# Layer 0's gate and up projections by seven block products instead of eight, and the down projection in groups of three tiles

## The chip, the cores and the metric

The kernel runs on one core of one Trainium2 chip. The metric is the device time of one execution in microseconds, the median of three runs. The engines are TensorE (PE, the matmuls), VectorE (DVE), ScalarE (ACT), GpSimd (POOL) and SyncE (SP), whose queue starts the DMA transfers.

## What is computed

Two layers of a diffusion backbone on 512 latent tokens (x) and 256 context tokens (ctx), 1024 features, all in fp32. Layer 0 is an RG-LRU and short-convolution mixer and a ConvFFN, on both streams; layer 1 is a neighbourhood attention and a ConvFFN, on x. The part that is changed is layer 0's ConvFFN; its input is a modulated copy of each stream, and its result is gated by a modulation vector:

```python
m_x = [t[:, None, :] for t in jnp.split(sc_c @ mod_w[i] + mod_b[i], 6, axis=-1)]
...
def conv_ffn(h, w_gate, w_up, conv_w, conv_b, w_down):
    g = dwconv(h @ w_gate, conv_w, conv_b, FFN_CONV // 2, FFN_CONV // 2)
    return (jax.nn.silu(g) * (h @ w_up)) @ w_down
```

`w_gate` and `w_up` are 1024 x 2816, `w_down` is 2816 x 1024, the convolution is over three neighbouring tokens and per feature. `mod_w` is 1024 x 6144 per layer: 24 chunks of 256 columns, times a vector for x and one for ctx.

## The kernel before, in words

**Products.** Activations lie with features on partitions and tokens on the free axis: 768 columns, x (XS, 512) before ctx (CS, 256). Every product in fp32 is three matmuls of rounded parts (`mm3`, lines 300 to 303): high weights by high activations, high by low, low by high. Of activations `hh` and `hl` are the high and the low part, of an FFN tile's result the two halves of `a`.

**Weights.** All weights are a list of units in the order of use (`unit`, `dma_to`, `split_w`, `split_to`, `use`, lines 109 to 167). A unit is loaded by SP into one of three raw buffers (`raw`, 128x1024), cast to its high part `wh` by ACT (L129), and the low part `wl` is the difference, taken by DVE (L130). There are four pairs of `wh` and `wl`. A load is issued as soon as the unit three before it has been split. Only SP's order is that of the code; the other engines' orders are set by a scheduler when the program is built.

**Layer 0's FFN.** The 2816 inner features are 22 tiles of 128 (f0 to f21). `ffn0_tile` (from line 848) does one: the gate's product (8 blocks of 128 rows x 3 matmuls, of 512 and of 256 columns), the convolution (ACT L838, DVE L839 and L840 from PSUM), silu (L841), the up product and the multiplication with it (L860), and the split of the result into `a` (ACT L845, DVE L846). Tiles 0 and 1 run apart, under the layer norm that precedes. The tiles are grouped, `FG0 = [7, 5, 3, 7]`: when a group and one more tile are done, the group's rows of `w_down` are multiplied for all eight panels of 128 output features, and `resid` (L731) adds each into the residual. The last group goes by column segments through `passes`, so that the next layer norm can start.

**Modulation.** The chunks are computed beside other work. `mod_step` (from line 200) does single steps: DVE multiplies 128x256 weights by a vector and adds (L220, L222); for ctx, where it is needed (all of layer 0, chunks 0 to 7 of layer 1), ACT multiplies (L224) and POOL adds (L226). PE then transposes the sums (L197), DVE reduces (L189). `mod_pe` (from line 252) does a chunk on PE instead, with the weights as the moving side (L240) and two transposes (L262); it serves in the mixer, with buffers of its own (`a`, L277). `mod_q` is the list of chunks that are still to do. In the kernel before, layer 0's chunks 8 to 19 go through `mod_pe` in the mixer, its chunks 20 to 23 and all 24 of layer 1 through `mod_step` in the FFN.

**Mixer.** For j = 0 to 3 it takes five products in the order sg, gates, sx, gr, sb, then the output projection. `seven_tile` and its helpers exist only after the change.

## Time and profile before

| what | value |
|---|---|
| median of 3 runs | 1605.63 us (1604.83 to 1608.91) |
| the profiled execution | 1607.75 us, its span 1605.9 us |
| mean granted TensorE clock | 0.996 |
| layer 0's FFN, tile 3 to the last down group | 371 to 822 us |
| last down group, norms, first projections of layer 1 | 822 to 930 us |
| attention | 930 to 1190 us |
| layer 1's output projection, norms and FFN | 1200 to 1606 us |

The span runs from the first instruction to the last. Busy time is time in which an engine has an instruction running; the matmuls overlap in the records, so their cadence is read from their starts. Where PE is busy for a whole stretch, only less work on PE shortens it. The stretches were found by the tiles' names in the timeline.

### The profile page before, as it was taken

The numbers are of one execution on the slowest core, as the hardware profiler recorded it, in microseconds if no ns is written. First come the engines' busy times: TensorE is split into PE (matmuls) and PEld (weight loads), VectorE is DVE, ScalarE is ACT, GpSimd is POOL, SyncE is SP. The second block draws the span as 40 slices with busy tenths as digits, with TensorE's granted clock in tenths as the row PEclk, the third lists the DMA queues.
The fourth block names the chain that finished last, engine by engine and source line by source line (L and its number), as shares of the span: only waits on it lengthen the run. The fifth ranks groups of instructions, "written<-read, shape, count | busy, mean of one in ns | idle before, by whom it ended". The sixth has DMA issues, their size and how long they took to land.

```text
span 1605.9 us, 24813 instructions
## 1 busy us (share of the span) xinstructions
PE 1560.7 (97%) x9630; PEld 1383.0 (86%) x9630; DVE 1050.3 (65%) x1899; ACT 757.5 (47%) x1329; POOL 297.2 (19%) x319
## 2 busy tenths in 40 slices
...
GB/s 280 248 146 100 151 79 145 157 77 171 138 112 135 134 111 160 121 165 87 60 104 143 104 79 66 53 73 44 50 150 120 100 94 95 92 92 105 99 99 53
DMA packets 284086, 184.27 MB, mean 115 GB/s; under 512 B 6720, under 2 KB 273344, under 8 KB 283968
## 3 DMA queue, kind: packets, MB, share of 16 engines
...
HBM read 180.56 MB, written 2.10 MB: 114 GB/s over the span
## 4 chain that ended last, share of the span: by engine, by line
PE 86%; DVE 4%; POOL 3%; ACT 2%; DMA 2%; issue 2%; SPq 0%; POOLq 0%; ACTq 0%; DVEq 0%
PE ps L302 22%; PE ps L301 22%; PE ps L303 22%; PE ps L1421 2%; PE ps L1423 2%; PE ps L1422 2%; PE ps L1059 2%; POOL sq L773 2%; PE ps L959 1%; PE ps L960 1%; PE ps L958 1%; DMA xk<-in_x_dram 1%; PE ps L240 1%; PE ps L1081 1%; PE ps L1074 1%
## 5 line engine op out<-in xcount | busy, mean ns | idle before, releaser
L301 PE MATMUL ps<-hh,wh 128*128 128x256 f32 (+1 forms) x1200 | 402.7, 336 | 0.0
L302 PE MATMUL ps<-hl,wh 128*128 128x256 f32 (+1 forms) x1200 | 400.4, 334 | 0.2 <-DVE hl L795 0.2
L303 PE MATMUL ps<-hh,wl 128*128 128x256 f32 (+1 forms) x1200 | 400.1, 334 | 0.3 <-DVE wl L130 0.3
L129 ACT CAST wh<-raw 128x1024 fp32r<-128x1024 f32 (+5 forms) x214 | 209.8, 983 | 370.4 <-PE ps L302 245.8
L130 DVE TENSOR_TENSOR wl<-raw,wh 128x1024 fp32r<-128x1024 f32 (+5 forms) x214 | 257.1, 1203 | 101.3 <-ACT wh L129 100.2
L301 PEld LDWEIGHTS ps<-hh,wh 128*128 128x128 f32 x1200 | 228.3, 190 | 25.7 <-issue 2.9
L303 PEld LDWEIGHTS ps<-hh,wl 128*128 128x128 f32 x1200 | 228.4, 190 | 23.2 <-DVE wl L130 0.5
L302 PEld LDWEIGHTS ps<-hl,wh 128*128 128x128 f32 x1200 | 228.5, 190 | 22.4 <-DVE hl L795 0.6
L301 PE MATMUL ps<-a,wh 128*128 128x256 f32 (+1 forms) x632 | 196.8, 312 | 0.2 <-ACT a L660 0.2
L302 PE MATMUL ps<-a,wh 128*128 128x256 f32 (+1 forms) x632 | 194.5, 308 | 0.7 <-DVE a L662 0.7
L303 PE MATMUL ps<-a,wl 128*128 128x256 f32 (+1 forms) x632 | 194.2, 307 | 0.8 <-DVE wl L130 0.7
L301 PE MATMUL ps<-h1h,wh 128*128 128x512 f32 (+1 forms) x384 | 142.2, 373 | 2.0 <-ACT h1h L792 2.0
L302 PE MATMUL ps<-h1l,wh 128*128 128x512 f32 (+1 forms) x384 | 142.0, 372 | 0.3 <-DVE h1l L795 0.2
L303 PE MATMUL ps<-h1h,wl 128*128 128x512 f32 (+1 forms) x384 | 142.0, 371 | 0.0
L303 PEld LDWEIGHTS ps<-a,wl 128*128 128x128 f32 x632 | 121.2, 192 | 7.0 <-DVE wl L130 1.4
L301 PEld LDWEIGHTS ps<-a,wh 128*128 128x128 f32 x632 | 121.3, 192 | 6.9 <-ACT wh L129 0.8
L302 PEld LDWEIGHTS ps<-a,wh 128*128 128x128 f32 x632 | 121.3, 192 | 5.9 <-DVE a L662 0.9
L222 DVE SCALAR_TENSOR_TENSOR mr<-mw,svec,mr 128x256 f32<-128x256 f32 x196 | 110.5, 567 | 3.7
L226 POOL TENSOR_TENSOR mr<-mr,mw 128x256 f32<-128x256 f32 x84 | 72.2, 860 | 111.8 <-ACT mw L224 106.0
L1046 POOL TENSOR_SCALAR s<-s,sm 128x512 f32<-128x512 f32 x64 | 47.8, 749 | 215.8 <-DVE sm L1045 196.7
L301 PEld LDWEIGHTS ps<-h1h,wh 128*128 128x128 f32 x384 | 71.9, 188 | 14.6 <-ACT h1h L792 2.1
L302 PEld LDWEIGHTS ps<-h1l,wh 128*128 128x128 f32 x384 | 72.0, 188 | 13.3 <-DVE h1l L795 0.9
...
## 6 DMA issues: line engine op xcount, KB each, us to landing
raw<-in_w_gate_dram SPq DMA_DIRECT2D x44, 512.0 KB, 4.3
raw<-in_w_up_dram SPq DMA_DIRECT2D x44, 512.0 KB, 4.0
...
a<-in_mod_w_dram SPq DMA_DIRECT2D x24, 512.0 KB, 5.2
raw<-in_w_out_dram SPq DMA_DIRECT2D x24, 512.0 KB, 4.2
raw<-in_w_qkv_dram SPq DMA_DIRECT2D x24, 512.0 KB, 3.8
raw<-in_w_down_dram SPq DMA_DIRECT2D x22, 512.0 KB, 3.6
```

Of the source, the lines that this page charges most:

```text
L129: nc.scalar.copy(h[:, :k], raw)
L130: nc.vector.tensor_tensor(out=l[:, :k], in0=raw, in1=f(h[:, :k]), op=ALU.subtract)
L222: stt(out=a[:, 0, :], in0=w, scalar=svec[:, k, 0:1], in1=a[:, 0, :], op0=ALU.mult, op1=ALU.add)
L226: G.tensor_tensor(out=a[:, 1, :], in0=a[:, 1, :], in1=w, op=ALU.add)
L301: mm(acc, wh, rh, start=first, stop=False)
L302: mm(acc, wh, rl, start=False, stop=False)
L303: mm(acc, wl, rh, start=False, stop=last)
L773: G.tensor_tensor(out=sq[0], in0=sq[0], in1=sq.pop(m - 1), op=ALU.add)
L1046: G.tensor_scalar(out=s, in0=s, scalar1=sm[:, 2:3], scalar2=0.0, op0=ALU.mult, op1=ALU.add)
L1059: nc.tensor.transpose(p[:, 128 * j:128 * j + 128], s[:, 128 * i:128 * i + 128], ident)
L1421: mm(p, ah, u["h"][:, k % 2, :], start=k == 0, stop=False)
L1422: mm(p, ah, u["l"][:, k % 2, :], start=False, stop=False)
```

## The change

**Seven products.** From tile 3 (`SW0`) on, a tile's gate and up products are taken as one block product: two halves of the 1024 input features, two outputs (gate and up), two halves of 384 tokens (`NH`). Eight block products give that plainly; Winograd's form of Strassen's method needs seven, of sums of blocks. Each is four `mm3` with 384 columns.

- Sums of weights are made by POOL (`sums_up`, L374 to L377) in four adds of 128x512, in place in the gate's and up's raw buffers and in `z`; two more units per tile, without a load, are split from them (512 and 1024 columns). The gate's raw buffer is held (`held=3`) until the last of them is split.
- Sums of activations are made once (`seven_acts`) in tiles 0 to 2: POOL adds high and low parts, DVE takes sums and low parts, ACT casts.
- The seven products are put together by DVE (L1043, seven adds of 128x384) and one ACT copy (L1045) into `g` and `up`.
- Convolution, silu and the product with `up` (`tail0`, from L1068) come one tile later, from SBUF, the product on POOL (L1084).

**Down groups.** `FG0 = [3, 3, 3, 3, 3, 7]`; a unit of `w_down` holds three blocks of 256 columns, two panels. In the last group the first three ctx panels do all tiles but the last first (`heads`).

**Modulation.** Chunks 20 to 23 of layer 0 go to PE in the mixer's last block (j = 3), their weights through the raw buffers; chunks 16 to 23 of layer 1 go into the attention loop.

```diff
-FG0 = [7, 5, 3, 7]
+FG0 = [3, 3, 3, 3, 3, 7]
+SW0 = 3
+NH = T // 2
...
+    def mod_unit(l, i, q):
+
+        unit(mod_w[l, q * 512:(q + 1) * 512, i * 256:(i + 1) * 256].rearrange("(k p) c -> p k c", p=128), 4, 256, held=1 << 20)
+        units[-1]["plain"] = True
...
-        while state["dma"] < min(n, len(units)) and state["dma"] - 3 < state["split"]:
+        while state["dma"] < min(n, len(units)):
             u = units[state["dma"]]
-            t = rawp.tile([128, 1024], F32, tag="raw", name="raw")
-            u["raw"] = t[:, :u["a"] * u["b"]].rearrange("p (a b) -> p a b", b=u["b"])
-            nc.sync.dma_start(out=u["raw"], in_=u["src"])
+            if u["src"] is not None:
+                if len(loaded) >= 3 and loaded[-3]["rel"] >= state["split"]:
+                    break
+                t = rawp.tile([128, 1024], F32, tag="raw", name="raw")
+                u["raw"] = t[:, :u["a"] * u["b"]].rearrange("p (a b) -> p a b", b=u["b"])
+                nc.sync.dma_start(out=u["raw"], in_=u["src"])
+                loaded.append(u)
...
+            if j == 3:
+                for q in range(2):
+                    mod_unit(0, 20 + LASTMOD.index(k), q)
...
+        def sums_up(u):
+            g = units[i]
+            z = Tp.tile([128, 512], F32, tag="mr", name="z", bufs=2)
+            units[i + 2]["raw"] = z.rearrange("p (a b) -> p a b", b=128)
+            G.tensor_tensor(out=z, in0=quarter(u, 0), in1=quarter(u, 1), op=ALU.add)
+            G.tensor_tensor(out=quarter(u, 0), in0=quarter(g, 0), in1=quarter(u, 0), op=ALU.subtract)
+            G.tensor_tensor(out=quarter(g, 0), in0=z, in1=quarter(g, 0), op=ALU.subtract)
+            G.tensor_tensor(out=quarter(g, 1), in0=quarter(g, 1), in1=quarter(g, 0), op=ALU.subtract)
+            units[i + 3]["raw"] = g["raw"]
+
+        for w, held, make in ((w_gate, 3, None), (w_up, 0, sums_up)):
+            unit(w[l][:, t * 128:(t + 1) * 128].rearrange("(k p) c -> p k c", p=128), KT, 128, make=make, held=held)
+        unit(None, 4, 128)
+        unit(None, KT, 128)
...
-        for sg in SEGS if gi == len(groups0) - 1 else ((CS, XS),):
-            for m in range(8):
-                order1.append(("d", gi, m, sg))
+        if gi < len(groups0) - 1:
+            order1 += [("d", gi, m) for m in range(0, 8, 2)]
+        else:
+            order1 += [("e", gi, m) for _ in SEGS for m in range(8)]
     for o in order1:
         if o[0] == "f":
-            gu_units(0, o[1])
+            (gu_units if o[1] < SW0 else seven_units)(0, o[1])
+            continue
+        a, n = groups0[o[1]]
+        if o[0] == "d":
+            unit(w_down[0][a * 128:(a + n) * 128, o[2] * 128:(o[2] + 2) * 128].rearrange("(k p) c -> p k c", p=128), n, 256)
...
+        if j < 3:
+            mod_pe(not (k == "sb" and j > 1))
+        else:
+            mod_raw(use(2, la=1))
...
+    gate_cols(0, 5, 5)
...
+                    for q, k in enumerate(order[:-1]):
+                        mm3(p[:, 0:s[1] - s[0]], u["h"][:, k, :], u["l"][:, k, :], rh(k, *s), rl(k, *s), q == 0, False)
+                    heads[m] = u, p
+                    if m == 0:
+                        last()
...
+        for k in range(4):
+            fa, fb = Tt("fa"), Tt("fb")
+            G.tensor_tensor(out=fa, in0=f(hh[:, k, :]), in1=f(hl[:, k, :]), op=ALU.add)
+            G.tensor_tensor(out=fb, in0=f(hh[:, k + 4, :]), in1=f(hl[:, k + 4, :]), op=ALU.add)
+            tt(out=t1[:, k, :], in0=fa[:, hi], in1=fa[:, lo], op=ALU.subtract)
+            tt(out=fa[:, hi], in0=fb[:, hi], in1=fa[:, hi], op=ALU.subtract)
+            tt(out=fb[:, hi], in0=fb[:, hi], in1=t1[:, k, :], op=ALU.subtract)
+            tt(out=fb[:, lo], in0=fb[:, lo], in1=fb[:, hi], op=ALU.subtract)
+            for j, src in ((3, fa[:, hi]), (2, fb[:, hi]), (4, fb[:, lo])):
+                nc.scalar.copy(dst(j, 0, k), src)
+                tt(out=dst(j, 1, k), in0=src, in1=f(dst(j, 0, k)), op=ALU.subtract)
+            yield
...
-    mod_q.extend([(0, i, 0) for i in range(20, 24)] + [(1, i, 0) for i in range(24)])
-    ring1 = (3, lambda: Tt("mw"), 3)
+    mod_q.extend((1, i, 0) for i in range(16))
+    ring1 = (2, lambda: Tt("mw"), 3)
...
+        def product(u, q, j):
+            p = bank()[:, 0:n]
+            for k in range(4):
+                mm3(p, u["h"][:, 4 * q + k, :], u["l"][:, 4 * q + k, :], B[j](0, k), B[j](1, k), k == 0, k == 3)
+            return p
+
+        def add(o, x, y):
+            tt(out=o, in0=x, in1=y, op=ALU.add)
+
+        nc.scalar.copy(g[:, lo], product(ua, 0, "11"))
+        split_to(i0 + 4)
+        between(0)
+        p3 = product(ub, 0, 3)
+        between(1)
+        p1 = product(ud, 0, 1)
+        split_to(i0 + 5)
+        between(2)
+        add(g[:, hi], product(uc, 0, 2), g[:, lo])
+        add(up[:, lo], p3, g[:, hi])
+        add(up[:, hi], p1, up[:, lo])
+        add(g[:, hi], p1, g[:, hi])
+        between(3)
+        add(g[:, lo], product(ua, 1, "21"), g[:, lo])
+        split_to(i0 + 6)
+        between(4)
+        add(up[:, lo], product(ub, 1, 4), up[:, lo])
+        split_to(i0 + 7)
+        between(5)
+        add(g[:, hi], product(uc, 1, "22"), g[:, hi])
+        between(6)
...
+    def tail0(t, g, up, segs=(XS, CS)):
+        tap = Tt("tap")
+        if len(segs) == 2 and segs[0] == XS:
+            act(out=tap, in_=g, func=AF.Identity, scale=col("fcw0", 22 + t), bias=col("fcb0", t))
+        else:
+            for o, e in segs:
+                act(out=tap[:, o:e], in_=g[:, o:e], func=AF.Identity, scale=col("fcw0", 22 + t), bias=col("fcb0", t))
+        yield
+        for k, (do, so) in ((0, (1, 0)), (44, (0, 1))):
+            for o, e in segs:
+                stt(out=tap[:, o + do:e - so], in0=g[:, o + so:e - do], scalar=col("fcw0", k + t), in1=tap[:, o + do:e - so], op0=ALU.mult, op1=ALU.add)
...
+            act(out=tap[:, o:e], in_=tap[:, o:e], func=AF.Silu)
+        yield
+        for o, e in parts:
+            (G if segs[0] == XS else V).tensor_tensor(out=up[:, o:e], in0=tap[:, o:e], in1=up[:, o:e], op=ALU.mult)
+        yield
+        a = atile[t] = ytile()
+        for o, e in parts:
+            nc.scalar.copy(a[:, 0, o:e], up[:, o:e])
+            tt(out=a[:, 1, o:e], in0=up[:, o:e], in1=f(a[:, 0, o:e]), op=ALU.subtract)
...
+            if not (t == NF - 2 and tail_at[0] == 5):
+                tail_step(1)
+                tail_at[0] += 1
+            if i % 2 == 0 and i < 6:
+                mod_step(1, *ring1)
...
+            u = use(la=2 if it[2] == 6 else 1)
+            for j in range(2):
+                ps_ = proj({"a": n, "h": u["h"][:, :, 128 * j:128 * j + 128], "l": u["l"][:, :, 128 * j:128 * j + 128]}, (CS, XS),
+                           lambda k, o, e: atile[a0 + k][:, 0, o:e], lambda k, o, e: atile[a0 + k][:, 1, o:e])
+                tail_step(2)
+                mod_step(2, *ring1)
+                for s, p in zip((CS, XS), ps_):
+                    resid(it[2] + j, s, 5, p)
...
-    gate_cols(1, 5, 5)
-    vecs(0, 1, col("g1_1", 0, 8), col("b1_1", 0, 8), 1, 3, 1)
...
+    mod_mem[0] = lambda: mop.tile([128, 1, 256], F32, tag="ma", name="ma", bufs=1)
+    ring2 = (1, lambda: mop.tile([128, 512], F32, tag="mw", name="mw", bufs=1), 2)
+    mod_q.extend((1, i, 0) for i in range(16, 24))
...
+            mod_step(1 + (n % 4 == 0), *ring2)
...
+    mods_flush()
+    gate_cols(1, 5, 5)
+    vecs(0, 1, col("g1_1", 0, 8), col("b1_1", 0, 8), 1, 3, 1)
```

**DVE, in a tile of layer 0's FFN.** First the kernel before, one tile from the gate's convolution to the next tile's split (`wl`: low part of weights, `ps`: PSUM, `tap`: the tile's gate):

```order
L839 SCALAR_TENSOR_TENSOR tap_5386<-ps_5393,colt_72,tap_5386 128x511
L840 SCALAR_TENSOR_TENSOR tap_5386<-ps_5393,colt_72,tap_5386 128x511
L839 SCALAR_TENSOR_TENSOR tap_5386<-ps_5418,colt_72,tap_5386 128x255
L840 SCALAR_TENSOR_TENSOR tap_5386<-ps_5418,colt_72,tap_5386 128x255
L130 TENSOR_TENSOR wl_5621<-raw_5391,wh_5620 128x1024
L860 TENSOR_TENSOR tap_5386<-tap_5386,ps_5473 128x512
L860 TENSOR_TENSOR tap_5386<-tap_5386,ps_5498 128x256
L189 TENSOR_REDUCE M1_77<-ps_5523 128x4
L220 TENSOR_SCALAR mr_5604<-mw_5457,svec_75 128x256
L248 SCALAR_TENSOR_TENSOR M1_77<-M1_77,colt_72 128x4
L130 TENSOR_TENSOR wl_5695<-raw_5471,wh_5694 128x1024
L846 TENSOR_TENSOR a_5539<-tap_5386,a_5539 128x768
```

After the change, a seven-product tile that follows another (`g_5229` and `up_5230` are its outputs; `raw_5192` and `raw_5249` hold the gate and up weights of the tile after it, `a_5367` is the result of the tile before it). All subtractions of L148 belong to the next tile:

```order
L148 TENSOR_TENSOR wl_5287<-raw_5192,wh_5286 128x1024
L268 SCALAR_TENSOR_TENSOR M1_77<-M1_77,colt_72 128x4
L1043 TENSOR_TENSOR g_5229<-ps_5300,g_5229 128x384
L1089 TENSOR_TENSOR a_5367<-up_5089,a_5367 128x768
L1043 TENSOR_TENSOR up_5230<-ps_5258,g_5229 128x384
L1043 TENSOR_TENSOR up_5230<-ps_5273,up_5230 128x384
L1043 TENSOR_TENSOR g_5229<-ps_5273,g_5229 128x384
L1043 TENSOR_TENSOR g_5229<-ps_5318,g_5229 128x384
L148 TENSOR_TENSOR wl_5338<-raw_5249,wh_5337 128x1024
L1043 TENSOR_TENSOR up_5230<-ps_5349,up_5230 128x384
L148 TENSOR_TENSOR wl_5364<-z_5332,wh_5363 128x512
L1043 TENSOR_TENSOR g_5229<-ps_5370,g_5229 128x384
```

A tile now has four weight subtractions where it had two, and the next up weights' low part (`wl_5338`) stands behind five adds and the low part of `a`; the fourth subtraction follows right after these rows.

**POOL, in the same stage.** Before, only modulation adds:

```order
L226 TENSOR_TENSOR mr_5142<-mr_5142,mw_5015 128x256 x2
L226 TENSOR_TENSOR mr_5142<-mr_5142,mw_5080 128x256 x3
L226 TENSOR_TENSOR mr_5142<-mr_5142,mw_5140 128x256 x2
L226 TENSOR_TENSOR mr_5290<-mr_5290,mw_5208 128x256 x2
L226 TENSOR_TENSOR mr_5290<-mr_5290,mw_5280 128x256 x3
```

After the change, around one seven-product tile (`up_4367` is the product of a tile's tail, `z` and `raw` are sums of weights):

```order
L1084 TENSOR_TENSOR up_4367<-tap_4529,up_4367 128x768
L374 TENSOR_TENSOR z_4610<-raw_4527 128x512
L375 TENSOR_TENSOR raw_4527<-raw_4470,raw_4527 128x512
L245 TENSOR_TENSOR mr_4575<-mr_4575,mw_4534 128x256
L376 TENSOR_TENSOR raw_4470<-z_4610,raw_4470 128x512
L245 TENSOR_TENSOR mr_4575<-mr_4575,mw_4534 128x256
L377 TENSOR_TENSOR raw_4470<-raw_4470 128x512
L245 TENSOR_TENSOR mr_4575<-mr_4575,mw_4534 128x256
L1084 TENSOR_TENSOR up_4508<-tap_4686,up_4508 128x768
```

The weight sums stand between a tail's product and the next one, and modulation adds between them.

**SP, at the end of the mixer (j = 3).** Before, the chunks' weights (`a`) come between the panels of `w_in` up to chunk 19, and the queue ends with three panels:

```order
L120 DMA raw<-in_w_in_dram 128x8x128
L277 DMA a<-in_mod_w_dram 128x4x256 x2
L120 DMA raw<-in_w_in_dram 128x8x128
L120 DMA raw<-in_gates_dram 128x512
L277 DMA a<-in_mod_w_dram 128x4x256 x2
L120 DMA raw<-in_w_in_dram 128x8x128
L277 DMA a<-in_mod_w_dram 128x4x256 x2
L120 DMA raw<-in_w_in_dram 128x8x128 x2
L120 DMA raw<-in_w_out_dram 128x8x128 x24
```

After the change:

```order
L133 DMA raw<-in_mod_w_dram 128x4x256
L304 DMA a<-in_mod_w_dram 128x4x256 x2
L133 DMA raw<-in_mod_w_dram 128x4x256
L304 DMA a<-in_mod_w_dram 128x4x256 x2
L133 DMA raw<-in_gates_dram 128x512
L133 DMA raw<-in_w_in_dram 128x8x128
L133 DMA raw<-in_mod_w_dram 128x4x256 x2
L133 DMA raw<-in_w_in_dram 128x8x128
L133 DMA raw<-in_mod_w_dram 128x4x256 x2
L133 DMA raw<-in_w_in_dram 128x8x128
L133 DMA raw<-in_mod_w_dram 128x4x256 x2
L133 DMA raw<-in_w_out_dram 128x8x128 x24
```

Between the last panels of `w_in`, and ahead of `w_out`, stand eight loads of modulation weights into the same raw buffers.

## Rows read from the trace of the kernel before

**Rows 1.** The page: busy time of each engine.
```profile
PE 1560.7 (97%) x9630; PEld 1383.0 (86%) x9630; DVE 1050.3 (65%) x1899; ACT 757.5 (47%) x1329; POOL 297.2 (19%) x319
```

**Rows 2.** Windows: stretch, its length, busy us of each engine, clock, DMA share.
```profile
160.00:235.00 75.00, 74.35 (x462) 63.90 (x462) 44.53 (x69) 48.51 (x65) 12.32 (x6) 1.00 0.38 109
342.00:371.00 29.00, 29.00 (x201) 27.08 (x200) 20.77 (x30) 18.34 (x29) 7.72 (x10) 1.00 0.57 173
371.00:822.00 451.00, 451.00 (x2626) 399.43 (x2625) 296.43 (x524) 152.07 (x241) 65.33 (x77) 1.00 0.40 122
...
930.00:1190.00 260.00, 257.25 (x1784) 237.49 (x1783) 179.09 (x471) 177.45 (x422) 47.15 (x63) 1.00 0.24 70
```

**Rows 3.** PE timeline, a down panel: start, duration of one (overlapping), instruction.
```profile
500.02 0.39 PE L301 MATMUL ps<-a,wh 128*128 128x512 f32 x1
...
502.06 0.28 PE L301 MATMUL ps<-a,wh 128*128 128x256 f32 x1
...
504.58 0.40 PE L301 MATMUL ps<-a,wh 128*128 128x512 f32 x1
```

**Rows 4.** PE timeline, mixer: a modulation chunk by the row method.
```profile
172.56 0.38 PE L262 MATMUL ps<-ident,mrw 128*128 128x128 f32 x2
172.87 1.07 PE L240 MATMUL ps<-a,mvec 128*32 128x256 f32 x16
173.87 0.50 PE L301 MATMUL ps<-hh,wh 128*128 128x512 f32 x1
```

**Rows 5.** DVE timeline where POOL is idle: subtractions of 1024 and 768 columns.
```profile
662.67 1.22 DVE L130 TENSOR_TENSOR wl<-raw,wh 128x1024 fp32r<-128x1024 f32 x1
663.80 0.95 DVE L846 TENSOR_TENSOR a<-tap,a 128x768 fp32r<-128x768 f32 x1
```

**Rows 6.** POOL timeline, then DVE's over the same stretch.
```profile
367.28 10.51 POOL L226 TENSOR_TENSOR mr<-mr,mw 128x256 f32<-128x256 f32 x10 [1.36 <-ACT mw L224]
369.35 1.76 DVE L130 TENSOR_TENSOR wl<-raw,wh 128x1024 fp32r<-128x1024 f32 x1
371.04 1.84 DVE L222 SCALAR_TENSOR_TENSOR mr<-mw,svec,mr 128x256 f32<-128x256 f32 x2
...
375.38 1.81 DVE L130 TENSOR_TENSOR wl<-raw,wh 128x1024 fp32r<-128x1024 f32 x1 [1.18 <-ACT wh L129]
377.12 1.49 DVE L846 TENSOR_TENSOR a<-tap,a 128x768 fp32r<-128x768 f32 x1
```

**Rows 7.** Groups by line and shape: count, busy us, mean ns, idle before.
```profile
L222 DVE SCALAR_TENSOR_TENSOR mr<-mw,svec,mr 128x256 f32<-128x256 f32 x196 | 110.5, 567 | 3.7
...
L226 POOL TENSOR_TENSOR mr<-mr,mw 128x256 f32<-128x256 f32 x84 | 72.2, 860 | 111.8 <-ACT mw L224 106.0 <-POOL mr L226 0.4 <-DMA mw<-in_mod_w_dram 0.3
...
L129 ACT CAST wh<-raw 128x1024 fp32r<-128x1024 f32 x154 | 160.9, 1048 | 275.3 <-PE ps L302 163.4 <-PE ps L1423 77.1 <-issue 20.0
...
L840 DVE SCALAR_TENSOR_TENSOR tap<-ps,colt,tap 128x511 f32<-128x511 f32 x44 | 32.9, 748 | 1.2
...
L586 POOL TENSOR_TENSOR ri<-ri,xc 128x768 f32<-128x768 f32 x8 | 14.8, 1846 | 139.2 <-ACT ri L629 139.0
...
L860 DVE TENSOR_TENSOR tap<-tap,ps 128x512 f32<-128x512 f32 x20 | 13.7, 683 | 22.4 <-PE ps L303 22.4
...
L840 DVE SCALAR_TENSOR_TENSOR tap<-ps,colt,tap 128x255 f32<-128x255 f32 x22 | 10.5, 479 | 0.4
...
L860 DVE TENSOR_TENSOR tap<-tap,ps 128x256 f32<-128x256 f32 x20 | 8.4, 420 | 34.0 <-PE ps L303 33.5 <-ACT mw L224 0.5
...
L1375 POOL TENSOR_TENSOR R<-R,gb 128x512 f32<-128x512 f32 x3 | 3.9, 1295 | 339.7 <-ACT R L1374 339.7
```

**Rows 8.** The page: DMA issues, KB each, median us to landing.
```profile
raw<-in_w_up_dram SPq DMA_DIRECT2D x44, 512.0 KB, 4.0
```

138 lines of the change are left out of this document (114 added, 24 removed).

## The prediction

> **What bounds the kernel now.** I read the page's busy line first, then the windows by stage, then single instructions. TensorE (PE) is busy 1560.7 of 1605.9 us [rows 1], so time goes only if PE gets less work, and comes back only if PE is made to wait. The windows show where there is room for waiting [rows 2]. From 371 to 822 us, which is layer 0's FFN from tile 3 to the start of its last down group, PE is busy 451.00 of 451.00 us. VectorE (DVE) is busy 296.4 of them, ScalarE (ACT) 152.1, GpSimd (POOL) 65.3. So the stage is PE's alone, with a third of DVE spare. In the attention (930 to 1190) PE has 257.3 of 260 us and DVE 179.1. The median of the three runs is 1605.63 us; the profiled run took 1607.75 us, 2.1 more. I make the sum against the profiled run and take 2.1 off at the end. About 0.3% (4.8 us) is what a measurement here can tell from no change.
>
> **What PE saves.** The cadence of matmuls is read from their starts [rows 3]. Nine of 512 columns start from 500.02 to 502.06: 0.2267 us each. The 21 of 256 columns from 502.06 to 504.58 take 0.120 each. A tile of gate and up has 48 of each: 48 x (0.2267 + 0.120) = 16.64 us. A seven-product tile has 7 x 4 x 3 = 84 matmuls of 384 columns. No 384 is in the trace. Priced per column like a 256 it takes 0.180, like a 512 0.170, and the mean of the two rows is 0.1734; I take the mean, since the row pair is a straight line with an offset, and 384 lies halfway. A tile is then 84 x 0.1734 = 14.57 us and saves 2.07; 19 tiles (3 to 21) save 39.3 us (ends: 28.9 and 44.8). The down products keep their number: 15 tiles x 8 panels x 3 x (0.2267 + 0.120) before and after.
>
> **What else moves on PE.** Twelve modulation chunks leave this stage. The four of layer 0, chunks 20 to 23, had 16 transposes here, the eight of layer 1, chunks 16 to 23, also 16; at 0.12 us, as for a matmul of 256, that is 3.8 us less. Four chunks go into the mixer's last block by the row method, 2 transposes 0.31 us and 16 narrow matmuls 1.00 us each [rows 4]: 4 x 1.31 = 5.2 more. The other eight take their 1.9 us into the attention. Net PE gain: 39.3 + 3.8 - 5.2 - 1.9 = 36.0 us. That is the gross term; the rest is what the new work makes PE wait.
>
> **The order on DVE inside a run of seven-product tiles.** This is the term I weigh most. DVE now splits four weight tiles per tile and adds seven products. Prices: the 1024 subtraction 1.22 us and the 768 subtraction 0.95 with POOL quiet [rows 5]; in a stretch where POOL ran ten adds back to back, 1.76 to 1.81 and 1.49 [rows 6]. An add of 384 from PSUM lies between 0.42 and 0.68 (256 and 512) [rows 7]: 0.55. In the order shown above, between the low parts of the next gate weights and of the next up weights stand an add, the previous tile's low part of 768, and four adds. There are four weight buffers, and the next gate weights take the one that product 5 reads. Set the tile's start to 0: product 5 ends at 5 x 2.08 = 10.4. The ACT cast takes 1.05 [rows 7], to 11.45; the gate's low part ends at 12.7, in time for 14.57. Then 0.55 + 0.95 + 4 x 0.55 + 1.22 brings the up weights' low part to 17.6. PE wants it in the third matmul of the next tile's product 2, at 14.57 + 2.08 + 0.35 = 17.0: 0.6 us late. At the prices with POOL busy the same walk ends at 19.2, 2.2 late. What is late there is late again at the next such boundary, since the walk starts from product 5. That order stands at seven boundaries (one in each of four runs of three, three in the last run); 1.3 each is 9 us, ends 4 and 15. Six boundaries without the 768 cost 0 to 0.7 each, 1 us together. I take 10 us.
>
> **Start of tile 3.** The sums of activations are new: POOL 8 adds of 128x768, DVE 32 passes of 384, ACT 16 casts, all in tiles 0 to 2. A 768 add on POOL takes 1.85 us [rows 7], so 14.8 us; 32 x 0.53 is 17 us of DVE. In 342 to 371, DVE has 8.2 of 29.0 us idle and POOL 21.3 [rows 2]. The work is spread over about two such windows, so the last sums should end near the start of tile 3, but POOL must then still make its four weight sums (4 x 1.3 us by the 512 add in [rows 7]) before products 2 to 4 of that tile. I take 6 us of PE waiting, ends 0 and 15.
>
> **The mixer's last block.** Each chunk's two 512 KB pieces now stand on the sync queue between the input panels, in three raw buffers, and are held until their rows are computed. A load lands in about 4 us [rows 8]; a panel lasts 24 x (0.2267 + 0.120) = 8.3 us of PE. That leaves one panel's time for two pieces and the next panel: tight, not late. The window is full now (74.35 of 75.0) [rows 2], so each late piece shows. I take 1.5 us, ends 0 and 6.
>
> **Attention.** Eight chunks bring 64 steps on DVE at 0.57 [rows 7], 36 us on 179 of 260. DVE is then at 83%, in a stage in which PE waits 2.7 us now. I take 3 us, ends 0 and 10. One microsecond more stands for the modulation columns and vectors that are now finished right behind the attention. The heads of the last down group (54 matmuls of 256, 6.5 us) cover tile 21's tail; a free cover, nothing in the sum.
>
> **Sum.** -36.0 + 10 + 6 + 1.5 + 3 + 1 = -14.5 us: 1607.75 - 14.5 = 1593.2 as a profiled run, about 1591 as the median.
>
> **POOL beside DVE.** What the rows show: in 367.28 to 377.79 POOL's ten adds and DVE's subtractions both ran, POOL at 1.05 us an add, DVE at 1.76 to 1.81 instead of 1.22 [rows 5, 6]. So the two slow each other, by 40 to 50%. The Trainium skill, "SBUF — State Buffer" (section "SBUF: two separate sides"), says that a DVE operation with two SBUF inputs and a GpSimd operation that reads SBUF take one port pair as an exclusive lock, and that the loser fully blocks. The rule speaks against this change, which gives POOL four weight sums and a product per tile; the sum by it would be that of the lesser form of rival 1, the sum by the rows is the one above. The trace agrees that the two lose together: in those 10.5 us POOL did ten adds (8.6 us at their mean of 0.86) and DVE two long subtractions and two modulation passes among others (2 x 1.22 + 2 x 0.57 = 3.6), more than fits one after the other. It does not show one engine standing still for all of the other's time.
>
> **Rivals.**
> 1. *The port shared by DVE and POOL makes DVE the bound (1605 to 1631 us; 18 in 100).* The place is three seven-product tiles and a down group, 3 x 14.57 + 24.9 = 68.6 us of PE. DVE alone: per tile 3 x 1.22 + 0.68 + 7 x 0.55 + 2 x (0.75 + 0.48) + 0.95 = 11.6; per down group 16 residuals, priced at 0.75 or 0.48 like the convolution's passes of about their widths, and four subtractions of 768, 13.6; 25 modulation steps at 0.57, 14 [rows 5, 7]. Together 62.5. Some 41 of that reads two operands from SBUF (subtractions 20, convolution 7, modulation 14). If all of it is stretched by 1.45 as in [rows 6], DVE needs 81, 12.4 us over PE in each of four cycles: 50 in place of the 10 above, and the time is 1591 + 40 = 1631. The point from which it decides: 0.3% slower than now needs 19 us more than I took, 29 in four cycles, so 76 us of DVE in a cycle, a stretch of 1.33. For it: the ratio itself is measured. Against it: POOL has work for only part of a cycle, 12 sums of 1.3 and three products of 1.85, 21 us; with some 19 modulation adds at 0.86 [rows 7], while layer 1's first eight chunks last, 37. That gives the lesser form: in some two and a half cycles the 41 us of DVE and the 37 of POOL take turns, 78 us, 9.4 over PE, 24 in all in place of the 10 above, and 1605.
> 2. *No new wait (about 1571 us; 19 in 100).* All of it hides: 1605.6 - 36.0 + 1. For it: DVE had 155 us to spare in the stage, and a stall at one boundary gives DVE time to catch up. Against it: the walk above, and that PE never waits in this stage now, so that any wait shows.
> 3. *Weights come late (about 1606 us; 8 in 100).* The gate's raw buffer is held until the fourth unit is split, so of three raw buffers only two turn over, and the up load starts some 6 us into the tile, lands 4 later [rows 8] and needs two POOL sums, cast and subtraction, 5 us, before 17.0. It fits by 2 us; a modulation load ahead of it on the queue takes that. Two us in each of 19 tiles give the whole gain back.
> 4. *The 384 matmul costs as much as the 512.* Then a tile takes 84 x 0.2267 = 19.0 us and the change loses 45. The two rows [rows 3] fall with the width, so I give this 1 in 100.
>
> **How the numbers follow.** The forecast (1581 to 1601) has 54 in 100: faster 50, within 0.3% 3, slower 1. Rival 1: 2, 8 and 8. Rival 2: 19 faster. Rivals 3 and 4: 0, 3 and 6. Faster 0.71, same 0.14, slower 0.15. The range goes from 1573, most of the way to rival 2, to 1613, past the lesser form of rival 1.
>
> **What would show it.** Matmuls of 384 columns starting 0.173 apart; tile starts 14.6 us apart where nothing waits; PE gaps of 1 to 2 us before the low-part matmul of product 2 (released by DVE, the subtraction) in the third tile of a run; a gap at tile 3's start released by POOL or DVE; DVE near 90% in the stage and subtractions nearer 1.4 than 1.2. I am wrong if tiles follow each other at 16 us or more throughout, if the gaps are released by DMA, or if the attention grows by more than 10 us.

## The result, and the profile after

The median of seven runs after the change is 1618.43 us (1612.66 to 1623.51), against 1605.63 before, also of seven: a ratio of 1.0077 (95% interval 1.0057 to 1.0097). It is slower, where I forecast 1591 in a range of 1573 to 1613. The profiled execution took 1617.7 us, 10 more than the profiled one of before, and it is compared here. First the busy line of the page after the change, which answers to [rows 1]:

```profile
PE 1541.6 (95%) x9458; PEld 1388.6 (86%) x9458; DVE 1193.9 (74%) x2067; ACT 779.5 (48%) x1331; POOL 452.5 (28%) x393
```

PE has 19 us less to do, DVE 144 more, POOL 155 more. The windows after the change (stretch, length, busy us of each engine, granted clock, DMA share and GB/s) show where PE waits; the last row answers to the stage's in [rows 2]:

```profile
378.00:390.00 12.00, 5.53 (x23) 3.72 (x21) 11.89 (x22) 6.19 (x13) 1.84 (x1) 0.75 0.31 98
390.00:400.00 10.00, 8.54 (x31) 7.93 (x32) 9.84 (x20) 7.01 (x14) 1.12 (x1) 0.62 0.01 2
400.00:640.00 240.00, 225.94 (x1274) 213.51 (x1273) 214.89 (x318) 99.29 (x150) 127.94 (x100) 0.96 0.34 104
505.00:515.00 10.00, 5.54 (x22) 4.80 (x23) 9.89 (x17) 3.57 (x8) 7.42 (x8) 0.66 0.29 92
...
371.00:822.00 451.00, 424.50 (x2384) 401.02 (x2383) 405.58 (x598) 177.58 (x252) 206.41 (x150) 0.97 0.33 100
```

In 371 to 822 us PE was busy without a gap; now it waits 26.5 us, with DVE at 90% and POOL at three times its former time. The starts of the matmuls divide the loss (us):

| stretch | before | after | change | predicted |
|---|---|---|---|---|
| first matmul of tile 3 | 370.92 | 378.00 | +7.1 | +6.7 |
| tile 3 to the last down group | 450.97 | 448.16 | -2.8 | -27.1 |
| last down group to the last matmul | 775.28 | 781.26 | +6.0 | +5.9 |

So the prediction's numbers held ahead of the stage and behind it, and missed by 24 us in it. Cut at the changes between tiles and down groups, the stage after the change is (us):

| f3 | d0 | f4-6 | d1 | f7-9 | d2 | f10-12 | d3 | f13-15 | d4 | f16-21 |
|---|---|---|---|---|---|---|---|---|---|---|
| 27.6 | 31.3 | 44.2 | 34.0 | 44.2 | 33.8 | 43.9 | 25.6 | 45.9 | 25.6 | 92.1 |

A tile needs 14.57 and a down group, as d3 and d4 show, 25.57. The runs of tiles lose 8.1 us together, tile 3 loses 13.0, and **the first three down groups lose 22.4**. The list of waits of PE from 366 to 830 us names the releasers (instruction that waited, releaser: us in total, times, longest):

```profile
PE ps L215 <- POOL mr L245: 11.0, 4, 4.0
PE ps L328 <- ACT a L976: 7.3, 3, 3.2
PE ps L330 <- DVE wl L148: 4.5, 6, 1.7
PE ps L215 <- DVE mr L241: 3.0, 3, 1.5
```

L215 is PE's transposes of a finished modulation chunk, which stand between down panels in PE's order. L245 is POOL's modulation add for ctx, L241 DVE's modulation pass, L148 DVE's weight subtraction, L976 the ACT casts of the sums of activations. The place is seen in d1; first PE's timeline (start, duration, instruction, idle before and its releaser):

```profile
503.56 0.39 PE L330 MATMUL ps<-a,wl 128*128 128x512 f32 x1
505.50 0.44 PE L215 MATMUL ps<-ident,mr 128*128 128x128 f32 x2 [1.55 <-DVE mr L241]
509.89 0.69 PE L215 MATMUL ps<-ident,mr 128*128 128x128 f32 x2 [3.96 <-POOL mr L245]
510.23 0.56 PE L328 MATMUL ps<-a,wh 128*128 128x256 f32 x1
```

Then POOL's over the same stretch:

```profile
500.33 1.29 POOL L374 TENSOR_TENSOR z<-raw 128x512 f32<-128x512 f32 x1
501.58 0.73 POOL L245 TENSOR_TENSOR mr<-mr,mw 128x256 f32<-128x256 f32 x1
502.27 1.48 POOL L375 TENSOR_TENSOR raw<-raw 128x512 f32<-128x512 f32 x1
503.83 1.33 POOL L376 TENSOR_TENSOR raw<-z,raw 128x512 f32<-128x512 f32 x1
505.24 1.33 POOL L377 TENSOR_TENSOR raw<-raw 128x512 f32<-128x512 f32 x1
506.53 3.31 POOL L245 TENSOR_TENSOR mr<-mr,mw 128x256 f32<-128x256 f32 x3
```

The chunk's last three adds wait on POOL behind four weight sums, and PE waits for them; the next down panel stands behind the transposes and starts 0.34 us after them. A wait also costs afterwards. At the granted 0.62 of 390 to 400 us, the lower of the clock's two levels (1.2 GHz) for most of it, matmuls of 384 columns start 0.31 to 0.37 us apart, not 0.1735:

```profile
394.88 0.52 PE L328 MATMUL ps<-hh,wh 128*128 128x384 f32 x1
395.19 0.56 PE L329 MATMUL ps<-hl,wh 128*128 128x384 f32 x1
395.56 0.52 PE L330 MATMUL ps<-hh,wl 128*128 128x384 f32 x1
395.88 0.52 PE L328 MATMUL ps<-hh,wh 128*128 128x384 f32 x1
```

The last ctx panel of d0, behind a wait of 1.81 us, took 1.86 us from its first start to its last, elsewhere 0.95. The windows of the first three down groups (stretch, length, busy us of PE, granted clock, DMA share and GB/s) divide their loss:

```profile
405.56:436.88 31.32, 28.04 (x153) 0.95 0.46 141
481.09:515.04 33.95, 28.39 (x153) 0.90 0.48 141
559.22:593.05 33.83, 28.61 (x154) 0.90 0.49 142
```

Of the 22.4 us PE is idle for 14.1 (3.3, 5.6 and 5.2). The other 8.3 pass while it is busy, about what the granted clocks of 0.95, 0.90 and 0.90 take from these lengths. So 3 to 6 us of waiting in a group cost 2.5 to 3 us more.

Where DVE and POOL both have work, their records show a lock step. POOL's timeline at the start of tile 3, sums of activations:

```profile
366.42 2.16 POOL L969 TENSOR_TENSOR fa<-hh,hl 128x768 f32<-128x768 f32 x1
368.54 2.16 POOL L970 TENSOR_TENSOR fb<-hh,hl 128x768 f32<-128x768 f32 x1
370.66 2.15 POOL L969 TENSOR_TENSOR fa<-hh,hl 128x768 f32<-128x768 f32 x1
...
377.02 2.83 POOL L970 TENSOR_TENSOR fb<-hh,hl 128x768 f32<-128x768 f32 x1
```

DVE's timeline, the same stretch:

```profile
366.80 2.20 DVE L977 TENSOR_TENSOR a<-fa,a 128x384 fp32r<-128x384 f32 x1
368.92 2.20 DVE L974 TENSOR_TENSOR fb<-fb 128x384 f32<-128x384 f32 x1
371.04 2.19 DVE L977 TENSOR_TENSOR a<-fb,a 128x384 fp32r<-128x384 f32 x1
373.16 0.74 DVE L921 SCALAR_TENSOR_TENSOR tap<-ps,colt,tap 128x511 f32<-128x511 f32 x1
...
375.28 2.87 DVE L148 TENSOR_TENSOR wl<-raw,wh 128x1024 fp32r<-128x1024 f32 x1
...
382.19 0.54 DVE L977 TENSOR_TENSOR a<-fa,a 128x384 fp32r<-128x384 f32 x1
```

A pass of 384 that takes 0.54 us at 382.19 takes 2.20, one for each POOL add, in step with it. The pass at 373.16, with one input from PSUM, keeps its 0.74.

### The profile page after: what moved, and what is told of

Read it like the earlier page. It is cut to its first block, busy times and chain, and to the rows that moved or that the text cites. A ratio compares the mean times of both kernels' runs of the same rounds, so it can differ in the third digit from the quotient of the medians.

```text
span 1615.9 us, 24708 instructions
## 1 busy us (share of the span) xinstructions
PE 1541.6 (95%) x9458; PEld 1388.6 (86%) x9458; DVE 1193.9 (74%) x2067; ACT 779.5 (48%) x1331; POOL 452.5 (28%) x393
## 4 chain that ended last, share of the span: by engine, by line
PE 42%; DVE 7%; POOL 2%; ACT 2%; issue 1%; DMA 1%; POOLq 0%; ACTq 0%; DVEq 0%; SPq 0%
PE ps L329 8%; PE ps L330 8%; PE ps L328 8%; PE ps L1662 2%; PE ps L1663 2%; PE ps L1661 2%; DVE wl L148 2%; PE ps L1293 2%; PE ps L1193 1%; PE ps L1194 1%; PE ps L1192 1%; PE ps L1308 1%; PE ps L1315 1%; POOL sq L837 1%; DVE tap L1077 1%
## 5 line engine op out<-in xcount | busy, mean ns | idle before, releaser
L147 ACT CAST wh<-raw 128x1024 fp32r<-128x1024 f32 (+3 forms) x229 | 228.8, 1003 | 317.4 <-PE ps L329 129.1
L148 DVE TENSOR_TENSOR wl<-raw,wh 128x1024 fp32r<-128x1024 f32 (+3 forms) x229 | 288.3, 1262 | 106.3 <-ACT wh L147 104.7
L328 PE MATMUL ps<-hh,wh 128*128 128x256 f32 (+2 forms) x896 | 300.3, 336 | 0.0
L330 PE MATMUL ps<-hh,wl 128*128 128x256 f32 (+2 forms) x896 | 298.4, 333 | 0.3 <-DVE wl L148 0.3
L329 PE MATMUL ps<-hl,wh 128*128 128x256 f32 (+2 forms) x896 | 298.4, 333 | 0.2 <-DVE hl L859 0.2
L328 PE MATMUL ps<-a,wh 128*128 128x256 f32 (+2 forms) x784 | 251.8, 321 | 7.4 <-ACT a L976 7.3
L330 PE MATMUL ps<-a,wl 128*128 128x256 f32 (+2 forms) x784 | 247.4, 316 | 6.0 <-DVE wl L148 5.8
L329 PE MATMUL ps<-a,wh 128*128 128x256 f32 (+2 forms) x784 | 248.0, 316 | 1.0 <-DVE a L977 0.6
L329 PEld LDWEIGHTS ps<-hl,wh 128*128 128x128 f32 x896 | 171.3, 191 | 10.8 <-DVE hl L859 0.6
L330 PEld LDWEIGHTS ps<-hh,wl 128*128 128x128 f32 x896 | 171.1, 191 | 11.0 <-DVE wl L148 0.5
L328 PEld LDWEIGHTS ps<-a,wh 128*128 128x128 f32 x784 | 151.8, 194 | 16.4 <-ACT a L976 8.4
L329 PEld LDWEIGHTS ps<-a,wh 128*128 128x128 f32 x784 | 151.7, 193 | 7.3 <-DVE a L977 1.7
L1280 POOL TENSOR_SCALAR s<-s,sm 128x512 f32<-128x512 f32 x64 | 50.7, 792 | 216.8 <-DVE sm L1279 177.7
L241 DVE SCALAR_TENSOR_TENSOR mr<-mw,svec,mr 128x256 f32<-128x256 f32 x112 | 81.9, 731 | 9.8 <-DMA mw<-in_mod_w_dram 7.8
```

The source lines that it names most:

```text
L147: nc.scalar.copy(h[:, :k], raw)
L148: nc.vector.tensor_tensor(out=l[:, :k], in0=raw, in1=f(h[:, :k]), op=ALU.subtract)
L241: stt(out=a[:, 0, :], in0=w, scalar=svec[:, k, 0:1], in1=a[:, 0, :], op0=ALU.mult, op1=ALU.add)
L328: mm(acc, wh, rh, start=first, stop=False)
L329: mm(acc, wh, rl, start=False, stop=False)
L330: mm(acc, wl, rh, start=False, stop=last)
```

## The experiments

All are edits of the changed kernel. Each ratio is against the kernel before on the same chip, whose medians there were 1607.4 to 1608.1 us. Three theories stood against each other: that DVE and POOL block each other while both read from SBUF (in the expectations theory A, the port); POOL's occupation as such, with PE's transposes behind it in order (theory E); late loads of modulation weights (theory C). From most runs the segments of the table above are given, each from one profiled execution.

**1. Sums of activations on DVE.** POOL's part of the sums goes to DVE.

```diff
-            G.tensor_tensor(out=fa, in0=f(hh[:, k, :]), in1=f(hl[:, k, :]), op=ALU.add)
-            G.tensor_tensor(out=fb, in0=f(hh[:, k + 4, :]), in1=f(hl[:, k + 4, :]), op=ALU.add)
+            tt(out=fa, in0=f(hh[:, k, :]), in1=f(hl[:, k, :]), op=ALU.add)
+            tt(out=fb, in0=f(hh[:, k + 4, :]), in1=f(hl[:, k + 4, :]), op=ALU.add)
```

> The eight adds of 128x768 that rebuild the activations before tile 3 go from POOL to DVE, nothing else. Changed kernel: tile 3 takes 27.6 us (378.0 to 405.6) where 14.6 are needed, and just before it DVE passes of 384 columns take 2.2 us each while POOL's adds run. Theory A (the port that DVE and POOL share blocks DVE for the whole of each POOL add): DVE gets 8 x 0.95 = 7.6 us more to do and no longer waits some 10 us; tile 3 falls to 17 to 21 us and the time by 6 to 11 us, to about 1610. Theory B (there is too much DVE work before tile 3, blocked or not): tile 3 stays at 27 us or grows towards 33, the time is 1618 to 1625.

Ratio 1.0057 (1.0039 to 1.0075), 1616.24 us. Tile 3 falls from 27.6 to about 20 us, and PE's wait for L976 from 7.3 to 1.8. The groups of DVE from 355 to 400 us (line, shapes, count, busy us, mean ns) show the passes free again, and what moved over:

```profile
L970 DVE TENSOR_TENSOR fb<-hh,hl 128x768 f32<-128x768 f32 x3 | 2.9, 955 | 0.0
...
L971 DVE TENSOR_TENSOR a<-fa 128x384 f32<-128x384 f32 x4 | 2.2, 556 | 0.0
```

After the change L971 had a mean of 1165 ns at this place. DVE does four times two 768 adds (0.955 us each) and is still earlier. But the down groups stay at 30.5, 34.2 and 34.5 us, the run f4-6 rises to 47.8, and at the end only 2 us are left of the 7 gained, less than the two ratios' intervals can tell apart. Theory A had the place right and the gain too high (6 to 11 us).

**2. Without the ctx adds on POOL.** Chunks 0 to 7 keep only the first of ACT's products.

```diff
-            if both(l, i):
-                act(out=a[:, 1, :] if k == 0 else w, in_=w, func=AF.Copy, scale=svec[:, k, 1:2])
-                if k:
-                    G.tensor_tensor(out=a[:, 1, :], in0=a[:, 1, :], in1=w, op=ALU.add)
+            if both(l, i) and k == 0:
+                act(out=a[:, 1, :], in_=w, func=AF.Copy, scale=svec[:, k, 1:2])
```

> Leaves out seven of the eight context steps of layer 1's modulation chunks 0 to 7: their ACT products and all POOL modulation adds of layer 0's FFN. Changed kernel: the first three down groups take 31.3, 33.9 and 33.8 us, the last two 25.6. Theory A (POOL with its weight sums and modulation adds, in turns with DVE's two-input passes, is too slow; PE's transposes of the context sums wait for it): all five groups take 25 to 26 us, the time falls by 20 to 25 us to about 1595. Theory C (modulation weights land late, behind weight loads on the sync queue): DVE's steps come as late as before and the first pair of transposes still waits; the groups stay at 28 to 32 us, the time falls by no more than 10.

Ratio 0.9965 (0.9949 to 0.9982), 1602.30 us. The down groups are 26.0, 26.0, 26.3, 25.6 and 25.6 us: the time lost there hangs on these adds and ACT's products for them. The whole falls by 16 us, where theory A had 20 to 25. It does not say how, through the port or through POOL's order.

**3. Modulation loads on ACT's queue.**

```diff
-            nc.sync.dma_start(out=t, in_=mod_w[...])
+            (nc.scalar if l and i < 16 else nc.sync).dma_start(out=t, in_=mod_w[...])
```

> The loads of layer 1's modulation weights, chunks 0 to 15, are issued from ACT's queue in place of the sync queue, where they stand behind weight loads that wait for raw buffers. Theory C (late loads are the cause): the first down groups fall from 31 to 34 us to 26 to 28, the time by 12 to 20 us. Theory A (POOL and DVE taking turns): the groups stay within 2 us of 31.3, 33.9 and 33.8 and the time within 5 us of 1618, unless ACT, which now waits for free buffers, makes it longer.

Ratio 1.0066 (1.0049 to 1.0083), 1618.94 us: no change, down groups 31.7, 33.9, 34.3. It told little, since ACT's queue waits too: the first load for d1, a group that starts at 483.6 us here, was issued at 487.29 us and ACT could use it at 493.5, 9.9 us into the group, against 11.1 in the changed kernel. Late loads stayed open.

**4. Eight products.** The rest of the change alone: three modulation steps per tile, no sums of activations.

```diff
-SW0 = 3
+SW0 = NF
...
-        next(acts)
-        mod_step(2, *ring1)
+        mod_step(3, *ring1)
...
-    acts = seven_acts()
+    acts = iter(lambda: 0, 1)
```

> All tiles of layer 0's FFN by eight block products as before (no sums of activations or weights), with the rest of the change: groups of three, modulation moved, heads of the last group; three modulation steps per tile. Theory A (the stalls come from what the seven products put on POOL and DVE): no waits in the stage, tiles 16.7 us, down groups 25.5 us, tile 3 right after tile 2, and the time is that of before plus the 7 us by which tile 3 started later and some 4 us behind the attention: about 1614 to 1618. Theory D (groups of three and the moved modulation cause the waits by themselves): the first down groups take 30 us or more here too, and the time is 1630 or more.

Ratio 1.0058 (1.0043 to 1.0073), 1617.06 us. Down groups take 25.6 to 26.0 us, so a group of three is no cost by itself; a tile takes 16.8. The last group starts at 821.97 us, as before (821.89), and its end comes 8.8 later. Hence the rest of the change costs about 9 us, and the seven products, as made, brought nothing over eight.

**5. Chunks with and without ctx in turn.**

```diff
-    mod_q.extend((1, i, 0) for i in range(16))
+    mod_q.extend((1, i, 0) for p in range(8) for i in (p, 8 + p))
```

> Layer 1's modulation chunks in layer 0's FFN are taken in the order 0, 8, 1, 9, ... 7, 15 in place of 0 to 15, so that chunks with context sums (POOL adds) are spread over all five down groups. Nothing else. Theory A (in a cycle of three tiles and a down group DVE's two-input passes and POOL take turns at the port; 41 + 37 = 78 us with three context chunks, about 69 with half of them): the excess of the down groups over 25.6 us falls from 23 us in the first three to 5 to 12 us over all five, the time by 10 to 18 us, to 1600 to 1608. Theory E (each context chunk costs its wait wherever it stands, because PE's transposes stand behind its last POOL add): the excess is spread but stays 18 to 25 us, the time within 5 us of 1618.

Ratio 1.0086 (1.0071 to 1.0102), 1623.24 us. Now d1 and d3 take 33.2 and 33.4 us, d0, d2 and d4 26 to 27, and the run f10-12 takes 49.9: the wait goes where the adds go. Theory A had forecast that the groups' loss falls to 5 to 12 us; it is 18.0, and a run loses 6 on top. Theory E's 18 to 25 fits, though the time lies a little above its range.

**6. A third buffer for modulation weights.**

```diff
-    ring1 = (2, lambda: Tt("mw"), 3)
+    ring1 = (3, lambda: Tt("mw"), 3)
```

> Three buffers for modulation weights in layer 0's FFN in place of two, as the kernel before had, so that loads are issued earlier. Theory C (the first steps of a down group come 11 us into it because their weights land late, and the rest is late for that): the first three groups fall from 31 to 34 us to 26 to 30, the time by 8 to 18 us. Theories A and E (POOL is behind for its own work and order): the groups change by less than 2 us each.

Ratio 1.0027 (1.0007 to 1.0046), 1611.65 us, 6.8 less than the changed kernel. d1 and d2 fall to 27.2 and 28.5, while the run f7-9 rises to 51.1: steps that start earlier put less of POOL's work in the down groups and more in the tiles. In the first two cycles of a down group and the run behind it nothing is gained (77.2 and 78.3 us for 75.5 and 78.1). The gain is in the third (74.2 for 77.8) and in the runs behind it (44.0 and 89.5 for 45.9 and 92.1). None of the theories had forecast this pattern.

**7. Weight sums after POOL's adds.** In the down group the next tile's weights are asked for one panel later.

```diff
-            u = use(la=2 if it[2] == 6 else 1)
+            u = use(la=1)
```

> In the last unit of a down group only one unit is split ahead in place of two, so that POOL's weight sums for the next tile are put behind the group's modulation adds. Theory E (order on POOL: the transposes wait for adds that stand behind the sums): the 4.2 us waits of PE for POOL at the end of the second and third group vanish, and the next tile waits 2 to 4 us in its second product instead; the time falls by 3 to 10 us. Theory A (the amount of work at the port): the wait only moves, group and following tiles together stay within 2 us of 78, the time within 4 us of 1618.

Ratio 1.0085 (1.0068 to 1.0102), 1622.85 us. The groups fall to 27.3, 28.7, 28.7, the runs rise to 49.9, 52.4, 50.9. Group and run together are 77.2, 81.2 and 79.5 us where they were 75.5, 78.1 and 77.8. The other order moved much of the wait to the tiles and made it longer. Theory E had the time fall, theory A had 78 within 2.

**8. Chunks in turn and activation sums on DVE** (the edits of 5 and 1).

> The alternating chunks and the eight adds before tile 3 on DVE together. By theory A the two gains add: 8 us at tile 3 and 10 to 18 in the down groups, 1592 to 1603, level with or under the kernel before. By theory E: about 1612.

Ratio 1.0044 (1.0029 to 1.0059), 1614.32 us, near theory E's 1612. d1 and d3 stay at 31.3 and 31.6. So runs 5 and 8 go against the price of theory A: fewer ctx adds in a cycle did not make the cycle shorter in proportion.

**9. ctx chunks in the tiles only,** the others in the down groups, one more step per tile, three buffers.

```diff
-                if mod_acc:
+                if mod_acc or at_down[0] is not None and at_down[0] == (i < 8):
                     break
...
-    mod_q.extend((1, i, 0) for i in range(16))
+    mod_q.extend((1, i, 0) for i in (8, 9, 0, 1, 10, 11, 2, 12, 13, 3, 4, 14, 15, 5, 6, 7))
...
-            if i % 2 == 0 and i < 6:
+            if i % 2 == 0:
                 mod_step(1, *ring1)
```

> Three modulation buffers, and a chunk with context sums is begun only in a run of tiles, a chunk without only in a down group (order 8, 9, 0, 1, 10, 11, 2, ...), with four steps per tile in place of three. Theory F (it is the meeting of three things at the end of a down group, the context adds, the next tile's weight sums on POOL and PE's transposes in its queue, that costs the 23 us; in the middle of a run the same adds cost nothing): the five groups take 25.5 to 27 us, the runs of three 44 to 46, the last group starts 12 to 20 us earlier against tile 3, the time is 1598 to 1607. Theory A (amount of work at the port of DVE and POOL, wherever it stands): groups fall to 26 but runs with context adds grow to 48 to 52, the time stays 1612 to 1620.

Ratio 1.0094 (1.0077 to 1.0111), 1622.64 us. The groups take 25 to 28 us, the runs of three 44.6 to 49.9. The waits of PE from 406 to 830 us now begin with another releaser:

```profile
PE ps L331 <- DVE wl L148: 14.3, 9, 3.2
```

PE no longer waits for POOL itself, and DVE's weight subtractions take its place. Theory F, that the adds cost nothing in the middle of a run, is out.

**10 and 11.** Run 9 with the activation sums on DVE, and run 6 with them.

> As the run before, and the eight adds before tile 3 on DVE. Theory F: another 5 to 8 us, 1591 to 1601, under the kernel before. Theory A: 1605 to 1613.

> Three modulation buffers and the eight adds before tile 3 on DVE, chunks in the order of the changed kernel. If the two gains (6.8 us and 2 to 7.5 us) add: 1602 to 1609; the first down group is still 28 us or more.

Run 10: 1.0057 (1.0041 to 1.0073), 1617.39 us. Run 11: 0.9999 (0.9984 to 1.0013), 1607.37 us, the kernel before's time; d0 is 32.6, the next two 26.0 and 28.1, but the runs ahead of these two 50.7 and 51.9. Run 10 lies above the ranges of both of its theories.

**12. The attention's chunks without DVE's sums.**

```diff
-            else:
+            elif l == 0 or i < 16:
                 stt(out=a[:, 0, :], in0=w, scalar=svec[:, k, 0:1], in1=a[:, 0, :], op0=ALU.mult, op1=ALU.add)
```

> Leaves out seven of the eight steps of each of the eight modulation chunks in the attention loop (their DVE passes; loads, transposes and sums stay). Changed kernel: from the first product of the attention stage to its last 270.8 us, before 266.5. Theory G (DVE's steps delay the attention): 267 to 268.5, the time falls by 2 to 4 us. Theory H (it is the transposes on PE and what follows the loop): 270 to 271, the time within 1.5 us of 1618.

Ratio 1.0051 (1.0036 to 1.0066), 1616.10 us. From the first product of the attention to its last, before has 266.5 us, the change 270.8, this 268.0: the DVE steps cost some 3 us. The size is rough, since the other runs, in which nothing is changed in this stage, have 269.0 to 273.0.

**13. Fills in place of the ctx adds.** POOL stays as busy, in the same place of its order, but reads nothing from SBUF.

```diff
                 if k:
-                    G.tensor_tensor(out=a[:, 1, :], in0=a[:, 1, :], in1=w, op=ALU.add)
+                    for o in (w, a[:, 1, :], w):
+                        G.memset(o, 0.5)
```

> Leaves out seven of the eight context steps of layer 1's chunks 0 to 7 and puts three POOL fills of 128x256 in place of each add (3 x 0.32 us, about what an add takes here; two into the modulation weights behind ACT, one into the sum), so that POOL is as busy and PE's transposes still wait for it, but POOL reads no SBUF for them. Theory A (port): DVE's passes are not blocked; the 1024 subtraction falls from a mean of 1.53 to 1.35 in 400 to 640 us, the first three groups to 26 to 28 us, the time by 12 to 20 us. Theory E (POOL's time and PE's queue): the groups stay at 31 to 34 us, the time within 5 us of 1618.

Ratio 0.9966 (0.9950 to 0.9982), 1603.19 us, the time of run 2. The down groups are 26.0, 26.0, 27.1, 25.6, 25.6, the runs of three 44.9 to 47.0. The profiled execution, 1598.85 us, is the fastest of ten. Its window from 400 to 640 us, against the third row of the windows above:

```profile
400.00:640.00 240.00, 234.90 (x1358) 221.14 (x1357) 216.42 (x336) 102.80 (x151) 119.81 (x205) 1.00 0.38 114
```

POOL is busy 119.8 us against 127.9, PE's transposes still stand behind its fills, and PE is busy 9 us more. From 366 to 830 us none of PE's waits is released by POOL any more. The groups of DVE over that window, run 13 (line, shapes, count, busy us, mean ns, idle before):

```profile
L241 DVE SCALAR_TENSOR_TENSOR mr<-mw,svec,mr 128x256 f32<-128x256 f32 x74 | 51.3, 693 | 8.3 <-DMA mw<-in_mod_w_dram 7.1
L148 DVE TENSOR_TENSOR wl<-raw,wh 128x1024 fp32r<-128x1024 f32 x29 | 39.2, 1353 | 3.1 <-ACT wh L147 3.1
```

and of the changed kernel:

```profile
L241 DVE SCALAR_TENSOR_TENSOR mr<-mw,svec,mr 128x256 f32<-128x256 f32 x69 | 51.7, 749 | 7.3 <-DMA mw<-in_mod_w_dram 6.2
L148 DVE TENSOR_TENSOR wl<-raw,wh 128x1024 fp32r<-128x1024 f32 x27 | 41.2, 1527 | 8.1 <-ACT wh L147 7.9
...
L1043 DVE TENSOR_TENSOR g<-ps,g 128x384 f32<-128x384 f32 x40 | 21.1, 546 | 0.0
```

The subtraction falls from 1527 to 1353 ns, the multiply from 749 to 693, while POOL is nearly as busy. So most of the cost is not POOL's time as such, but that it reads from SBUF while DVE takes two operands from there. L1043, with one operand in PSUM, has in both the 0.55 us of its price.

**14 and 18, 15, 16. POOL's work moved to DVE,** on top of run 11: all four weight sums (14, and the same kernel again as 18), the first two (15), or the tail's product (16).

```diff
-            G.tensor_tensor(out=z, in0=quarter(u, 0), in1=quarter(u, 1), op=ALU.add)
+            tt(out=z, in0=quarter(u, 0), in1=quarter(u, 1), op=ALU.add)
...
-            (G if segs[0] == XS else V).tensor_tensor(out=up[:, o:e], in0=tap[:, o:e], in1=up[:, o:e], op=ALU.mult)
+            V.tensor_tensor(out=up[:, o:e], in0=tap[:, o:e], in1=up[:, o:e], op=ALU.mult)
```

> Third modulation buffer, the adds before tile 3 and all four weight sums of each tile on DVE. Port: POOL keeps 22 us a cycle, DVE's two-input passes grow from 41 to 49 (12 x 0.68): 71 in place of 78; DVE alone 62.5 + 8.2 = 70.7 against 68.6 of PE. Theory A: a cycle with context adds falls from 78 to 71 to 74, one without stays at 71 to 73, the time is 1594 to 1603. Theory E: DVE's extra work comes on top, 1610 to 1625.

> The kernel of e14 once more in five rounds, for a narrower interval: 1596 to 1602, a ratio of 0.992 to 0.997 against the kernel before.

> As the run before, but only the first two of the four sums (those that the second product waits for) on DVE. Theory A: halfway, 1599 to 1605; Theory E: 1607 to 1616.

> Third modulation buffer, the adds before tile 3 on DVE, and the product of a tile's tail (128x768) on DVE in place of POOL. Port: POOL loses 5.5 us a cycle, DVE gains 2.9. Theory A: 2 to 3 us less in each cycle with context adds, 1599 to 1605. Theory E: level with the run without it, 1607, or slower.

Run 14: 0.9942 (0.9921 to 0.9963), 1598.21 us; again as run 18: 0.9946 (0.9933 to 0.9960), 1599.22. Run 15: 0.9982 (0.9970 to 0.9995), 1604.96. Run 16: 0.9955 (0.9941 to 0.9969), 1602.66. All lie in the ranges of theory A. DVE is the busier engine, and more work on it makes the kernel faster.

**17. Sums and tail product on DVE** (14 and 16 together).

> All four weight sums and the tail's product on DVE together, with the third modulation buffer and the adds before tile 3 on DVE; POOL keeps only the context adds. Port: 52 us of DVE and 16 of POOL a cycle, 68; DVE alone 73.6 against 68.6 of PE. Theory A with DVE's own work as the next bound: cycles with context adds about 75, those without 70 to 74 (DVE alone), the time 1597 to 1605, no better than with the sums alone. If DVE's own work were no bound: 1590 to 1596.

**Ratio 0.9875 (0.9862 to 0.9889), 1587.94 us: faster than both kernels.** Its window and groups from 400 to 640 us:

```profile
400.00:640.00 240.00, 234.64 (x1345) 220.29 (x1344) 233.99 (x397) 103.29 (x151) 57.18 (x53) 0.99 0.38 116
```

```profile
L241 DVE SCALAR_TENSOR_TENSOR mr<-mw,svec,mr 128x256 f32<-128x256 f32 x77 | 41.1, 534 | 0.4
L148 DVE TENSOR_TENSOR wl<-raw,wh 128x1024 fp32r<-128x1024 f32 x29 | 37.3, 1285 | 1.5 <-ACT wh L147 1.5
...
L1084 DVE TENSOR_TENSOR up<-tap,up 128x768 f32<-128x768 f32 x10 | 9.6, 960 | 0.6 <-ACT tap L1081 0.4
```

DVE took over more than half of what POOL did and is busy 97.5% of the window, yet its subtraction is back at 1285 ns (alone 1.22 us [rows 5]) and its multiply at 534. The moved product takes 0.96 us on DVE, 1.94 on POOL. The first down group still takes 28.3 us and the second 30.0, the others 25.6 to 26.0; the runs of three take 44 to 46.2. I had expected DVE's own work to be the next bound here (1597 to 1605); the time came out under even the 1590 to 1596 for the case that it is none.

## Why the prediction was wrong

- **Gain on PE: right.** The matmul of 384 columns was priced at 0.1734 us by the mean of its neighbours [rows 3]. PE's timeline after the change:

```profile
442.98 0.33 PE L330 MATMUL ps<-hh,wl 128*128 128x384 f32 x1
443.15 0.33 PE L328 MATMUL ps<-a,wh 128*128 128x384 f32 x1
443.32 0.33 PE L329 MATMUL ps<-a,wh 128*128 128x384 f32 x1
443.50 0.33 PE L330 MATMUL ps<-a,wl 128*128 128x384 f32 x1
443.67 0.33 PE L328 MATMUL ps<-a,wh 128*128 128x384 f32 x1
```

Four steps in 0.69 us. A run of three tiles in which PE never waits takes 43.9 us, 14.6 a tile. Rival 4 falls.
- **DVE order inside the runs: right in size, in good part by luck.** 10 us taken, 8.1 measured, of which the waits on L148 are 4.5. At the place of the walk, the third matmul of product 2, PE waits in tiles 15, 19, 20 and 21, but only 0.28 to 0.59 us each, 1.75 together, where I took 1.3 at each of seven boundaries. The other two waits, 1.09 and 1.67, are in product 4 of tiles 13 and 16, where DVE has the residuals of a down group and modulation passes ahead of the subtraction. The granted clock of the runs stays at 1.00, so the rest is no slow clock; it was not followed up.
- **Start of tile 3: too low, inside its ends.** Tile 3 lost 13.0 us, I took 6 of 0 to 15. The sum of 14.8 us for POOL and 17 for DVE was made as if the two ran beside each other.
- **Ahead of the stage and behind it: right in size, so close by luck.** +7.1 and +6.0 us where 6.7 and 5.9 were taken; the attention grew by 4.3, of which run 12 gives some 3 to DVE's steps. But in runs 14 and 18, one kernel, the start of tile 3 differs by 1.6 us and the time from the last down group to the last matmul by 5.8. In the mixer's window of [rows 2] PE stays full (75.0 of 75.0), so the 1.5 us for late pieces do not show there.
- **The failed step: down groups of three were priced at nothing.** I costed the products, which are as many as before, and nothing of what now stands beside them on POOL. They lost 22.4 us, 14.1 of them PE's waiting for the modulation sums in its order (11.0 of it released by POOL's ctx adds) and 8.3 slower matmuls. Against the stage's miss of 24 stand these 22.4, 7 more in tile 3, 2 less in the runs, and some 3 us by which PE's own need fell further than I counted; the last was not followed up.
- **Under it lies "POOL beside DVE".** I read [rows 6] as two engines that slow each other by 40 to 50%, and took the rows' price. The trace after shows a pass of 384 stretched fourfold, from 0.54 to 2.20. The Trainium skill, "SBUF — State Buffer" (section "SBUF: two separate sides"), has the pair as an exclusive lock for a whole instruction. By that rule a DVE pass and a POOL add take turns, and the trace after agrees in the main: one pass per add, every 2.12 us, where the two alone sum to 2.39 (0.54, and 1.85 [rows 7]). Its section "Who interferes with whom" says that a GpSimd instruction which only writes does not contend with such a pass; run 13 agrees, 1603.19 us against 1618.43. My sentence that the trace does not show one engine standing still holds only for the row that merges ten adds. The single adds of before, beside the last two rows of [rows 6], show turns:

```profile
375.37 0.74 POOL L226 TENSOR_TENSOR mr<-mr,mw 128x256 f32<-128x256 f32 x1
376.19 1.60 POOL L226 TENSOR_TENSOR mr<-mr,mw 128x256 f32<-128x256 f32 x1
```

DVE's subtraction, begun with the first add, ends 1.08 us after it; the second add ends 0.60 us after that subtraction, and DVE's pass of 768 ends 0.82 us after the second add. Each ends about its time alone (1.22, 0.74 and 0.95), less some 0.1 us, after the other is done. The mean of 0.86 us per add, on which I rested "more than fits one after the other", already held such waits: an add that is not held up takes 0.74, and with that the sum is 11.0 us against the stretch's 10.5.
- **Rival 1 came nearest,** with 1605 to 1631. Its lesser form has 78 us per cycle of run and group, computed from 41 us of DVE and 37 of POOL in turns. The cycles d0 to d2 with their runs measured 75.5, 78.1 and 77.8. That agreement is partly luck, since the slow clock behind each wait, which I had not priced, is in the measured ones. The same sum gave about 69 for run 5, and its first four cycles measured 72.0, 77.2, 76.1 and 77.3. That the engines take turns is shown; that their added times are the price of a cycle is not. I gave it 18 in 100 because POOL had work for part of a cycle only. That share is no argument where the engines take turns: their times add. Nor did I see that PE meets it in the down group, behind POOL's adds, and not in the tile.
- **Rival 3 (late weights) did not show.** No gap of PE in the stage was released by a load of tile weights. Late modulation weights, which it did not name, have a part: run 6 gains 6.8 us with a third buffer for them. Rival 2 fell; even run 17, at 1587.9, ends 17 us above its 1571.

Still open: how much of a down group's wait is POOL's slowness beside DVE and how much its order, since runs 5 and 8 fit theory E better and runs 13 to 16 theory A.
